# Two transformer blocks on one core: side steps after every three products, and another order of projections

## The chip, the cores and the metric

One core of one Trainium2 chip. The metric is the device time of one execution in microseconds, and lower is better. TensorE multiplies, VectorE and ScalarE work on vectors, SP issues transfers.

## The reference

Two blocks of two layers each, on 256 tokens of width 1024, in float32. Of the first block a layer is a mixer, cross attention with 256 memory rows, and a gated FFN; of the second, an FFN, a mixer with three attentions, and a second FFN. The part that the change is mostly about, cut:

```python
def second_block(x, ...):
    for l in range(DEPTH):
        h = rms_norm_2(x, ffn1_norm[l])
        x = x + 0.5 * swiglu_2(h, ffn1_w_gate[l], ffn1_w_up[l], ffn1_w_down[l])
        h = rms_norm_2(x, mix_norm[l])
        (nq, nkc, nvc, nks, nvs, nkw, nvw, ngate, sq, sk, sv, wq, wk, wv, bgate) = jnp.split(
            h @ w_in[l], SPLIT_POINTS, axis=-1)
        y_nsa = nsa_attention(...)          # sparse: compressed, selected and window branch, 8 heads
        y_sb = stick_breaking_attention(...)  # 4 heads
        y_swa = swa_sink_attention(...)       # sliding window of 128, 4 heads
        g = jax.nn.sigmoid(bgate).reshape(B, S, N_BRANCHES, D_MODEL)
        merged = (g[:, :, 0] * (y_nsa @ w_up_nsa[l]) + g[:, :, 1] * (y_sb @ w_up_sb[l])
                  + g[:, :, 2] * (y_swa @ w_up_swa[l]))
        x = x + merged @ w_out[l]
        h = rms_norm_2(x, ffn2_norm[l])
        x = x + 0.5 * swiglu_2(h, ffn2_w_gate[l], ffn2_w_up[l], ffn2_w_down[l])
    return x
```

In the first block, `parallel_mixer` joins a linear recurrence, a forgetting attention and a retention, all from one projection `h @ w_in`, and `memory_cross_attention` reads keys and values of the memory.

## The kernel before

**Products.** The large matrix products set the pace. Weights are streamed from memory in chunks of up to 1 MB by SP (three raw buffers, `raw`), and each chunk is split into pieces of at most 128x1024: ScalarE rounds a piece to `whi`, VectorE takes the difference `wlo` (six piece buffers). The activations are split alike (`thi`, `tlo`). One product is three matmuls into one PSUM bank, hi·hi, hi·lo and lo·hi, written by `mm3`; in this text a "product" is one such matmul, so `mm3` is three products. A piece in `mm_nat` gives 6 products for each of the two token tiles (two k tiles of 512 columns, or one of 1024), or 12 (four k tiles of 256 columns).

**Side steps.** Everything between the large products, the attentions, the recurrence, the transposes, is written as Python generators. `side(gen)` puts one on a list, and each `yield` ends one step, with the time at which its next one may begin. `pump()` goes through the list and emits the steps that are due, into the same instruction streams, where the program stands. A planner (`Pace`) keeps an estimate of when each engine is done; `pump` takes a step only when its time has come by that estimate (within 0.3 us) and one of two PSUM banks of the pool `aux` is free:

```python
due = [i for i in ready if i[1] <= nc.products + 0.3 and aux_free() <= nc.products + 0.3]
```

Where a product needs what a side step has yet to make, `need` and `finish` call `pump(force=True)`, which emits the next step whether its time has come or not. All engines work through their streams in order, so a side step's instructions stand in TensorE's stream between two products, and its vector work in the streams of VectorE and ScalarE between the splits of weights. The order is settled when the program is built, by the estimate.

**Where `pump()` stands before.** In `nat_blocks`, after every token tile of a piece, so mostly after 6 products; in `stat_block` (weights are the stationary operand there, 128x256 moving) in the middle of each piece and at its end; in `out_rows` after each piece and token tile; in the loop that makes the memory's keys and values (`fill_steps`) in the middle of a piece; in the `up` projections of the second mixer after a piece's second token tile only. The first pass of `nat_blocks` over token tile 0 (`skew`) and the last pieces of `out_rows` (`held`) have none.

**The second mixer.** Its input projection is done in column groups, each a call with a callback, and a callback starts the work on what has come: `nq` (queries of the sparse attention), `sqk` (stick-breaking queries and keys; starts `both`, that is `sb` and then `swa`), `svwq` (stick-breaking values and sliding queries), `nkv` (sparse keys and values for compression and selection; starts `compress_blocks`), `wkv` (sliding keys and values), `nwin` (window keys and values and the gates; starts `nsa`). Then follow the gate projections, between them the compression's matmuls (`compress_mm`, `o<-raw,t`), and three `up` projections. `nsa` has eight units of two heads; `pairs` runs the steps of each unit in turn: scores (`aux<-kT,qT`), softmax rows on VectorE and ScalarE (`rn`), their transposition (`aux<-ident,rn`), the output (`o<-rn,vsw`); after units 4 and 8 the compressed branch's part (`o<-bc,kk`). `swa` has the same steps under the names `wkT,wqT`, `rs`, `wv`. `compress_attention` makes `kc`, `kcb` and that part's probabilities. `ta`, `kk` hold normalised queries and keys on the way to their transposes. The third `up` projection needs the whole output of `nsa` from its third k tile on, the second that of `swa`, the first that of `sb`.

**Cross attention and first mixer** have side steps of their own: `cpr` (probabilities), `o<-cpt,mv` (output), `hk` (strips of the bias table for the second block, read back from memory by a transfer that a side step issues), `rot` (rotated queries), `o<-pt,fv` (forgetting attention).

Of the kernel before, what the change touches and what calls it, by code (L numbers as in the profile page):

```python
# [272 lines left out]
def tile_two_blocks(ctx, tc, I, out):  # L273
# [196 lines left out]
    def mm_nat(dst, T, t, piece, first, last):  # L470

        hi, lo, kts, _ = piece
        b = hi.shape[2]
        for j, kt in enumerate(kts):
            need(T, kt, t)
            xs = slice(t * P, (t + 1) * P)
            for c in range(0, b, 512):
                e = min(c + 512, b)
                mm3(dst(t, c, e), T.hi[:, kt, xs], T.lo[:, kt, xs], hi[:, j, c:e], lo[:, j, c:e],
                    first and j == 0, last and j == len(kts) - 1)  # L480

    def nat_blocks(T, blocks, skew=0, after=None):
# [6 lines left out]
        items = []  # L489
# [5 lines left out]
        def run(item, piece, t):  # L495
            i, n, cb, st = item
            if st["dst"] is None:
                st["dst"] = st["mk"]()
            mm_nat(st["dst"][0], T, t, piece, i == 0, i == n - 1)
            if t == 1 and i == n - 1 and cb:  # L500
                nc.end = nc.products
                cb(st["dst"][1])

        held = []
        for k in range(min(skew, len(items))):
            piece = W.take()
            run(items[k], piece, 0)
            held.append(piece)
            if k in T.late:
                T.late.pop(k)()  # L510
# [19 lines left out]
    def stat_block(T, npieces, ncb, cb, dst=None):  # L530

        a = dst if dst is not None else acc()
        for i in range(npieces):
            piece = W.take()
            hi, lo, kts, idx = piece
            for j, kt in enumerate(kts):
# [10 lines left out]
                if j + 1 == len(kts) // 2:  # L547
                    pump()
# [9 lines left out]
    def out_rows(kt_of, npieces, tail, chain, n_fill=0, both=False, head=0, late=None):  # L558
# [12 lines left out]
        def go(t, T, piece, first, last):  # L571
            mm_nat(dst, T, t, piece, first, last)
            if t == 1:
                W.done(piece[3])

        if head:
            some = [get(i) for i in range(head)]
            for t in (0, 1):
                for k, s in enumerate(some):
                    go(t, *s)  # L580
                    if late and t == 0 and k >= head - 2:
                        next(late)
                    pump()
        for i in range(head, npieces - tail):
            s = get(i)
            for t in (0, 1):
                go(t, *s)
# [603 lines left out]
    def fill_steps(n):  # L1191
# [3 lines left out]
        for l, kind, c in todo:  # L1195
            if kind == "k" or c % 2 == 0:
                a = acc()
            for i in (0, 1):
                hi, lo, kts, idx = W.take()
                for j, kt in enumerate(kts):  # L1200
                    if j == len(kts) // 2:
# [204 lines left out]
    def plan_mixer2(l):  # L1406
# [5 lines left out]
        nat(1304, 512)  # L1412
        nat(1816, 512)
        nat(512, 512)
        nat(2328, 256)
        nat(1024, 280)
# [11 lines left out]
    def mixer2(l, T, next_maker):  # L1428
        with nc.pool(tc, name=nm("mix2"), bufs=2) as mp:
# [426 lines left out]
            nat_blocks(T, [(4, dst_tiles, svwq_done), (4, dst_tiles, nkv_done), (2, dst_tiles, wkv_done), (4, dst_tiles, nwin_done)])  # L1856
# [5 lines left out]
            def up(kt0, n, g0, first):  # L1862
# [3 lines left out]
                for t in (0, 1):  # L1866
                    for i, (hi, lo, kts, idx) in enumerate(held):
                        mm_nat(dst, Y, t, (hi, lo, [kt0 + k for k in kts], idx), i == 0, i == n - 1)
# [201 lines left out]
```

## Time and profile before

| | |
|---|---|
| time, median of 3 runs | 2149.8 us (2143.81 to 2149.81) |
| profiled execution, own time | 2147.57 us |
| its span | 2145.8 us |
| TensorE busy | 2067.2 us (96%) |
| VectorE busy | 1250.7 us (58%) |
| ScalarE busy | 1096.1 us (51%) |
| mean granted clock of TensorE | 0.98 |
| transfers | 380.79 MB, 177 GB/s on the mean |

The own time of the profiled execution is the span of its records and 1.8 us around it. PE is TensorE's matrix multiplication, PEld its weight load, DVE VectorE, ACT ScalarE. [...] A wait is named by what ended it: "aux <- DVE rn" is a matmul into `aux` that waited for VectorE's writing of `rn`. Line L151 is that of the recorder through which the whole program goes; groups are told apart by their tiles.

### The profile page before, as it was taken

To read this page: it belongs to the slowest core of one execution; us is meant where nothing else is said; L and a number is where in the kernel's file an instruction comes from. 1 tells how busy PE (TensorE), PEld (TensorE's weight loads), DVE (VectorE), ACT (ScalarE), POOL (GpSimd) and SP (SyncE) were. 2 spreads that over 40 slices of the span, in tenths; PEclk is the share of its full clock that TensorE was granted. 3 is DMA by queue.
4 is the path that set the end of the run, shared out by engine and by line. 5 is a ranking of instruction groups with operands and counts; after the bars stand their busy time and mean duration, and the time that the engine had idled before them with its cause. 6 is when DMAs were issued, how large, how long until landed. Compare 5 with 4: busy or idle time off the path is not lost.

```text
span 2145.8 us, 27307 instructions
## 1 busy us (share of the span) xinstructions
PE 2067.2 (96%) x10446; PEld 1692.5 (79%) x10446; DVE 1250.7 (58%) x2123; ACT 1096.1 (51%) x1840; POOL 90.2 (4%) x112
## 2 busy tenths in 40 slices
PE   7999999999899999999999999999999998989999
PEld 6878788888787788788887667888888886768887
DVE  6666565556663655565465656664655565647563
ACT  5556465454554654555363545654554454446552
POOL 0210000001100000000000000000000000000000
PEclk9999999999999999999999999999999999989999
DMA  7555565655554555556536543555565547525553
GB/s 241 179 190 179 170 207 177 215 175 164 184 186 149 196 188 195 171 182 204 191 129 197 187 123 138 195 179 195 177 196 189 165 158 225 138 85 194 192 185 109
DMA packets 200610, 380.79 MB, mean 177 GB/s; under 512 B 14288, under 2 KB 70400, under 8 KB 200480
## 3 DMA queue, kind: packets, MB, share of 16 engines
q1 hardware_dynamic: 188960, 366.46, 51.9%
q10 hardware_dynamic: 11520, 12.59, 1.8%
q8 instruction: 82, 1.34, 0.2%
q14 instruction: 48, 0.39, 0.1%
HBM read 372.03 MB, written 6.99 MB: 177 GB/s over the span
## 4 chain that ended last, share of the span: by engine, by line
PE 83%; DVE 6%; ACT 4%; DMA 4%; issue 3%; POOL 1%; SPq 0%; ACTq 0%; DVEq 0%; POOLq 0%
PE acc L151 73%; PE aux L151 7%; DMA raw<-in_w_in_dram 2%; DVE wlo L151 2%; PE o L151 2%; ACT whi L151 1%; ACT rn L151 1%; ACT thi L151 1%; DVE h L151 0%; DMA mem<-in_mem_dram 0%; ACT cpr L151 0%; DMA nb<-cdram 0%; DVE ngm L151 0%; DVE tlo L151 0%; DMA bt<-btiles 0%
## 5 line engine op out<-in xcount | busy, mean ns | idle before, releaser
L151 PE MATMUL acc<-whi,thi 128*128 128x512 f32 (+1 forms) x1760 | 701.5, 399 | 10.8 <-ACT kvout L151 6.5
L151 PE MATMUL acc<-wlo,thi 128*128 128x512 f32 (+1 forms) x1760 | 685.1, 389 | 5.0 <-DVE wlo L151 4.7
L151 PE MATMUL acc<-whi,tlo 128*128 128x512 f32 (+1 forms) x1760 | 685.2, 389 | 2.5 <-DVE tlo L151 2.4
L151 DVE TENSOR_TENSOR wlo<-raw,whi 128x1024 fp32r<-128x1024 f32 (+1 forms) x370 | 442.3, 1208 | 302.1 <-ACT whi L151 300.4
L151 ACT CAST whi<-raw 128x1024 fp32r<-128x1024 f32 (+1 forms) x370 | 378.3, 1036 | 274.1 <-PE acc L151 221.7
L151 DVE SCALAR_TENSOR_TENSOR wlo<-raw,prm,whi 128x512 fp32r<-128x512 f32 (+1 forms) x592 | 392.3, 717 | 178.2 <-ACT whi L151 178.0
L151 ACT ACTIVATE whi<-raw,prm 128x512 fp32r<-128x512 f32 (+1 forms) x592 | 371.6, 694 | 93.3 <-PE acc L151 89.8
L151 PEld LDWEIGHTS acc<-whi,thi 128*128 128x128 f32 x1760 | 333.4, 189 | 88.1 <-issue 11.2
L151 PEld LDWEIGHTS acc<-whi,tlo 128*128 128x128 f32 x1760 | 332.6, 189 | 75.1 <-DVE tlo L151 7.1
L151 PEld LDWEIGHTS acc<-wlo,thi 128*128 128x128 f32 x1760 | 333.5, 189 | 71.4 <-DVE wlo L151 9.1
L151 PE MATMUL acc<-whi,ahi 128*128 128x512 f32 x528 | 206.8, 392 | 0.3
L151 PE MATMUL acc<-whi,alo 128*128 128x512 f32 x528 | 205.6, 389 | 0.0
L151 PE MATMUL acc<-wlo,ahi 128*128 128x512 f32 x528 | 205.5, 389 | 0.0
L151 POOL TENSOR_TENSOR r<-v,mhalf 128x1 f32<-128x1 f32 (+3 forms) x46 | 51.5, 1120 | 1619.5 <-DVE v L151 1619.5
L151 DVE SCALAR_TENSOR_TENSOR silu<-acc,r,silu 128x512 f32<-128x512 f32 (+1 forms) x72 | 47.5, 702 | 118.2 <-PE acc L151 94.2
L151 PEld LDWEIGHTS acc<-whi,ahi 128*128 128x128 f32 x528 | 99.1, 188 | 21.6 <-ACT whi L151 1.5
L151 PEld LDWEIGHTS acc<-whi,alo 128*128 128x128 f32 x528 | 99.1, 188 | 20.6
L151 PEld LDWEIGHTS acc<-wlo,ahi 128*128 128x128 f32 x528 | 99.2, 188 | 20.1
L151 PE MATMUL acc<-thi,whi 128*128 128x256 f32 x384 | 111.7, 291 | 0.0
L151 PE MATMUL acc<-tlo,whi 128*128 128x256 f32 x384 | 108.6, 283 | 0.0
L151 PE MATMUL acc<-thi,wlo 128*128 128x256 f32 x384 | 108.5, 283 | 0.0
L151 ACT ACTIVATE silu<-acc,r 128x512 f32<-128x512 f32 (+1 forms) x72 | 43.1, 650 | 127.7 <-PE acc L151 127.6
(299 smaller groups left out, 1857.1 us busy)
## 6 DMA issues: line engine op xcount, KB each, us to landing
raw<-in_w_in_dram SPq DMA_DIRECT2D x65, 1024.0 KB, 5.0
raw<-in_ffn_w_down_dram SPq DMA_DIRECT2D x44, 1024.0 KB, 4.8
raw<-in_ffn_w_gate_dram SPq DMA_DIRECT2D x40, 1024.0 KB, 5.0
raw<-in_ffn_w_up_dram SPq DMA_DIRECT2D x40, 1024.0 KB, 5.1
raw<-in_w_down_dram SPq DMA_DIRECT2D x22, 1024.0 KB, 4.9
raw<-in_w_gate_dram SPq DMA_DIRECT2D x20, 1024.0 KB, 5.0
raw<-in_w_up_dram SPq DMA_DIRECT2D x20, 1024.0 KB, 5.0
raw<-in_w_out_dram SPq DMA_DIRECT2D x16, 1024.0 KB, 4.9
```

Of the source, the lines that this page charges most:

```text
L151: return f(*args, **kwargs)
```

## The change

Two parts. First, `mm_nat` takes a flag `beside`, with which it calls `pump()` after each three products (not after the last of a piece, which has its own); `nat_blocks` sets it except in its first pass, `out_rows` for all but the held pieces, and `up` throughout. `stat_block` calls `pump()` after each two column blocks, which are six products, and `fill_steps` after each k tile but the last. Second, in the second mixer the projections follow in the order nq, sqk, nkv, nwin, svwq, wkv, instead of nq, sqk, svwq, nkv, wkv, nwin, in the plan of weights and in the calls alike.

```diff
-    def mm_nat(dst, T, t, piece, first, last):
+    def mm_nat(dst, T, t, piece, first, last, beside=False):
...
+        left = len(kts) * (-(-b // 512))
...
+                left -= 1
+                if beside and left:
+                    pump()
...
-        def run(item, piece, t):
+        def run(item, piece, t, beside=True):
...
-            mm_nat(st["dst"][0], T, t, piece, i == 0, i == n - 1)
+            mm_nat(st["dst"][0], T, t, piece, i == 0, i == n - 1, beside)
...
-            run(items[k], piece, 0)
+            run(items[k], piece, 0, False)
...
-                if j + 1 == len(kts) // 2:
-                    pump()
+                    if c % 2 == 1 and (j + 1 < len(kts) or c + 1 < ncb):
+                        pump()
...
-                    go(t, *s)
+                    go(t, *s, beside=True)
...
-                    if j == len(kts) // 2:
+                    if j:
                         pump()
...
+        nat(512, 512)
+        nat(1024, 280)
         nat(1816, 512)
-        nat(512, 512)
         nat(2328, 256)
-        nat(1024, 280)
...
-            nat_blocks(T, [(4, dst_tiles, svwq_done), (4, dst_tiles, nkv_done), (2, dst_tiles, wkv_done), (4, dst_tiles, nwin_done)])
+            nat_blocks(T, [(4, dst_tiles, nkv_done), (4, dst_tiles, nwin_done), (4, dst_tiles, svwq_done), (2, dst_tiles, wkv_done)])
...
-                        mm_nat(dst, Y, t, (hi, lo, [kt0 + k for k in kts], idx), i == 0, i == n - 1)
+                        mm_nat(dst, Y, t, (hi, lo, [kt0 + k for k in kts], idx), i == 0, i == n - 1, True)
```

What this does to the instructions at three places of the second mixer, layer 0. The first is TensorE's stream at the third `up` projection, ahead of its third k tile (`o` is the output of the sparse attention's second half, `acc` the projection). Before:

```order
L151 MATMUL acc_10772<-whi_10652,tlo_9145 128x512
L151 MATMUL aux_10790<-kT_9150,qT_9149 128x128
L151 MATMUL aux_10791<-kT_9150,qT_9149 128x128
L151 MATMUL aux_10790<-kT_9150,qT_9149 128x256
L151 MATMUL aux_10791<-kT_9150,qT_9149 128x256
L151 MATMUL o_10814<-rn_10766,vsw_9148 64x256
L151 MATMUL o_10814<-rn_10768,vsw_9148 64x256
L151 MATMUL o_10814<-rn_10766,vsw_9148 64x128
L151 MATMUL o_10814<-rn_10768,vsw_9148 64x128
L151 MATMUL aux_10819<-ident_90,rn_10798 128x128 x3
L151 MATMUL aux_10820<-ident_90,rn_10803 128x128 x3
```

After the last of these rows two more such units follow, down to the compressed part, before the next product. After the change the same place reads:

```order
L151 MATMUL acc_10889<-whi_10789,thi_9144 128x512
L151 MATMUL acc_10889<-wlo_10790,thi_9144 128x512
L151 MATMUL acc_10889<-whi_10789,tlo_9145 128x512
L151 MATMUL o_10662<-rn_10902,vsw_9148 64x256
L151 MATMUL o_10662<-rn_10904,vsw_9148 64x256
L151 MATMUL o_10662<-rn_10902,vsw_9148 64x128
L151 MATMUL o_10662<-rn_10904,vsw_9148 64x128
L151 MATMUL o_10662<-bc_10569,kk_10425 128x256 x2
L151 MATMUL acc_10889<-whi_10807,thi_9144 128x512
L151 MATMUL acc_10889<-wlo_10808,thi_9144 128x512
```

One output group with the compressed part stands there; the scores, turns and other outputs of these units stand between earlier products.

The second is TensorE's stream at `kc`, `kcb`, the normalised compressed keys, and the sliding attention's `rs`. Before:

```order
L151 MATMUL acc_10331<-whi_10195,thi_9144 128x512
L151 MATMUL acc_10331<-wlo_10196,thi_9144 128x512
L151 MATMUL acc_10331<-whi_10195,tlo_9145 128x512
L151 MATMUL aux_10379<-ident_90,kc_10320 128x30
L151 MATMUL aux_10387<-kcb_10381,qT_9149 128x30 x8
L151 MATMUL aux_10403<-ident_90,rs_10148 128x128 x3
L151 MATMUL aux_10404<-ident_90,rs_10153 128x128 x3
L151 MATMUL o_10250<-rs_10411,wv_9147 64x256
```

Nothing stood between them. After, at `kc` and at `kcb`, which are two pieces of one stream:

```order
L151 MATMUL aux_10456<-ident_90,kc_10428 128x30
L151 MATMUL acc_10322<-whi_10239,thi_8714 128x512
L151 MATMUL acc_10322<-wlo_10240,thi_8714 128x512
L151 MATMUL acc_10322<-whi_10239,tlo_8715 128x512
L151 MATMUL acc_10322<-whi_10239,thi_8714 128x512
L151 MATMUL acc_10322<-wlo_10240,thi_8714 128x512
L151 MATMUL acc_10322<-whi_10239,tlo_8715 128x512
```

```order
L151 MATMUL acc_10322<-whi_10277,thi_8714 128x512
L151 MATMUL acc_10322<-wlo_10278,thi_8714 128x512
L151 MATMUL acc_10322<-whi_10277,tlo_8715 128x512
L151 MATMUL aux_10478<-kcb_10458,qT_9149 128x30 x8
L151 MATMUL acc_10322<-whi_10277,thi_8714 128x512
```

There are 12 products from `kc` to `kcb`, and the groups of `rs` are elsewhere.

The third is VectorE's stream where the sliding attention's queries and keys are normalised (`ta`) ahead of their transposes, with the splits of weights `wlo` for the compress stretch. Before:

```order
L151 TENSOR_REDUCE s_798_9823<-t_795_9799 128x8
L151 TENSOR_SCALAR v_9826<-s_798_9823 128x8
L151 TENSOR_TENSOR wlo_9836<-raw_9797,whi_9835 128x1024
L151 TENSOR_TENSOR wlo_9852<-raw_9797,whi_9851 128x1024
L151 TENSOR_TENSOR ta_9776<-wqk_9491,r_793_9779 128x768
L151 TENSOR_TENSOR kk_9610<-kk_9610,r_799_9824 128x512
L151 TENSOR_SCALAR wqT_9151<-aux_9877,prm 128x2x128
L151 TENSOR_SCALAR wkT_9152<-aux_9877,prm 128x128
```

After:

```order
L151 TENSOR_SCALAR rn_9871<-rn_9871,nsum_9864 128x128
L151 TENSOR_SCALAR rn_9871<-rn_9871,nsum_9864 128x256
L151 TENSOR_TENSOR ta_9824<-wqk_9701,r_808_9827 128x768
L151 TENSOR_TENSOR wlo_9921<-raw_9883,whi_9920 128x1024
L151 TENSOR_SCALAR wqT_9151<-aux_9942,prm 128x2x128
L151 TENSOR_SCALAR wkT_9152<-aux_9942,prm 128x128
L151 TENSOR_TENSOR wlo_9955<-raw_9883,whi_9954 128x1024
```

The multiplication into `ta` stood behind two splits of one chunk and stands ahead of them now.

Counted over the whole program, places with side steps on TensorE's stream go from 239 to 276; in a second mixer, from 38 to 52 in each layer. Places where only three products separate two groups of side steps were none and are 11 in each second mixer, 3 and 5 in the first mixers. In an FFN one place moves by three products.

## Rows read from the trace of the kernel before

**Rows 1.** The page: the span, and busy time of each engine.

```profile
span 2145.8 us, 27307 instructions
...
PE 2067.2 (96%) x10446; PEld 1692.5 (79%) x10446; DVE 1250.7 (58%) x2123; ACT 1096.1 (51%) x1840; POOL 90.2 (4%) x112
```

**Rows 2.** Windows of eight stretches: busy time of each engine, granted clock, DMA.

```profile
696.00:885.80 189.80, 188.04 (x852) 154.01 (x851) 109.18 (x151) 100.90 (x155) 2.69 (x4) 1.00 0.56 186
1075.90:1325.60 249.70, 233.77 (x1258) 181.65 (x1258) 150.24 (x318) 121.04 (x232) 9.57 (x9) 0.95 0.49 156
1272.90:1294.90 22.00, 16.55 (x80) 9.75 (x78) 7.84 (x44) 9.10 (x32) 0.00 (x0) 0.69 0.05 16
1220.60:1232.40 11.80, 8.10 (x40) 6.49 (x38) 8.09 (x23) 2.14 (x5) 0.00 (x0) 0.67 0.29 91
1158.90:1166.30 7.40, 4.41 (x29) 1.90 (x27) 6.04 (x9) 2.50 (x3) 0.00 (x0) 0.78 0.67 223
1898.10:1921.40 23.30, 17.88 (x81) 10.54 (x79) 7.84 (x44) 9.15 (x32) 0.00 (x0) 0.63 0.05 14
582.50:592.50 10.00, 6.02 (x29) 3.60 (x27) 4.50 (x11) 3.71 (x9) 0.00 (x0) 0.69 0.32 122
659.70:672.10 12.40, 8.69 (x26) 5.70 (x24) 2.24 (x3) 2.72 (x5) 0.00 (x0) 0.72 0.70 233
```

**Rows 3.** Waits of TensorE by what ended them: us in total, times, longest.

```profile
PE aux L151 <- DVE rn L151: 9.3, 6, 2.3
...
PE aux L151 <- DVE ta L151: 6.0, 2, 3.0
PE aux L151 <- DVE kcb L151: 5.8, 2, 2.9
PE acc L151 <- DVE wlo L151: 4.7, 8, 0.8
PE aux L151 <- DVE cpr L151: 3.8, 2, 3.0
PE aux L151 <- DMA hk<-ud: 3.7, 1, 3.7
...
PE aux L151 <- ACT rs L151: 1.8, 2, 0.9
```

**Rows 4.** TensorE's timeline, end of the second mixer, layer 0: start, us, instruction.

```profile
1273.18 0.93 PE L151 MATMUL aux<-kT,qT 64*128 64x128 f32 x8
...
1277.18 1.16 PE L151 MATMUL aux<-ident,rn 128*128 128x128 f32 x6 [2.27 <-DVE rn L151]
...
1294.90 0.50 PE L151 MATMUL acc<-whi,thi 128*128 128x512 f32 x1 [0.68 <-ACT thi L151]
```

**Rows 5.** TensorE's timeline, second mixer, layer 0: three side groups between products.

```profile
1201.21 0.39 PE L151 MATMUL acc<-whi,tlo 128*128 128x512 f32 x1
1201.44 0.82 PE L151 MATMUL aux<-ident,rn 128*128 128x128 f32 x6
...
1202.33 0.39 PE L151 MATMUL acc<-wlo,thi 128*128 128x512 f32 x1
...
1209.18 0.39 PE L151 MATMUL acc<-whi,tlo 128*128 128x512 f32 x1
1209.50 0.93 PE L151 MATMUL aux<-kT,qT 64*128 64x128 f32 x8
...
1210.69 0.39 PE L151 MATMUL acc<-wlo,thi 128*128 128x512 f32 x1
...
1266.18 0.39 PE L151 MATMUL acc<-whi,tlo 128*128 128x512 f32 x1
1266.50 0.87 PE L151 MATMUL o<-rn,vsw 128*64 128x256 f32 x8
1267.30 1.13 PE L151 MATMUL o<-bc,kk 128*128 128x256 f32 x4
...
1268.50 0.40 PE L151 MATMUL acc<-wlo,thi 128*128 128x512 f32 x1
```

More of the change, by code (lines that the diff above doesn't have):

```diff
@@ L569, in get, with go @@
             return T, (hi, lo, [k - base for k in kts], idx), i == 0, i == npieces - 1
-        def go(t, T, piece, first, last):
-            mm_nat(dst, T, t, piece, first, last)
+        def go(t, T, piece, first, last, beside=False):
+            mm_nat(dst, T, t, piece, first, last, beside)
             if t == 1:
@@ L586, in out_rows @@
             for t in (0, 1):
-                go(t, *s)
+                go(t, *s, beside=True)
                 pump()
```

## The prediction

> **What bounds the kernel now.** Read the page first [rows 1]: TensorE is busy 2067.2 of 2145.8 us, so 78.6 us of the span are waits, and the rest can only shrink where TensorE ran at its lower clock. The question is then where these two lie. The windows [rows 2] answer it. In an FFN stretch (the first row) TensorE is busy 188.04 of 189.80 us at a granted clock of 1.00: nothing to win. In the second mixer of block two (second row) it is busy 233.77 of 249.70 at 0.95, and the rows of short stretches below it say which parts lower that mean: 22.0 us at 0.69, 11.8 at 0.67, 7.4 at 0.78 and, in layer 1, 23.3 at 0.63. In each of these stretches no product runs: several side steps stand one behind the other, and TensorE waits between them for the step before. [...] The list of TensorE's waits [rows 3] names the same places: 9.3 us for `rn` (rows of scores after the softmax, on VectorE), 6.0 for `ta`, 5.8 for `kcb`, 3.8 for `cpr`, 3.7 for a transfer of `hk`. The timeline of the 22 us stretch [rows 4] shows one such wait: the scores start at 1273.18, their transpose can only start at 1277.18 after 2.27 us idle, and the first product comes back at 1294.90.
>
> So the bound is TensorE, and what can be won is waiting for chains VectorE–ScalarE–TensorE that have no products to cover them.
>
> **The change, part by part.** No matmul is removed. It makes more places where side steps may stand, and it brings the sparse attention's inputs forward by one or two projections (sqk, then nkv and nwin before svwq and wkv). The order of the instructions says what becomes of the stretches.
>
> *End of the second mixer.* Before, the last `up` projection, at its third k tile, needs what four units of the sparse attention have still to give, and ten groups are forced there in a row; after, only the last output group stands there (the rows are in the part on the change). At full clock, what stays of the stretch is its matmuls. Their price is read where such groups stand between products at full clock [rows 5]: time from the last product before to the second product behind, less two pitches of a product (1201.44 less 1201.21, 0.23). Scores: 1210.69 − 1209.18 − 0.46 = 1.05. Turns: 1202.33 − 1201.21 − 0.46 = 0.66. Output with the compressed part: 1268.50 − 1266.18 − 0.46 = 1.86. For an output group alone I take the price of the scores, which have as many matmuls: 1.05. The stretch has 3 scores, 3 turns, 4 outputs, one of them with the compressed part: 3 × 1.05 + 3 × 0.66 + 3 × 1.05 + 1.86 = 10.1 us. These stay, elsewhere. So does the wait of 0.68 for `thi` at its end [rows 4]. Gain: 22.0 − 10.1 − 0.7 = 11.2 in layer 0 and 23.3 − 10.1 − 0.7 = 12.5 in layer 1: **23.7**.
>
> *Compressed attention* (one place before, with `kc`, `kcb`, two groups of the sliding attention's `rs` and one of `rn`; `kc` and `kcb` stand apart after). For this and the next stretches I take busy time times granted clock as the work that stays [rows 2]; on the stretch above that gives 16.55 × 0.69 = 11.4 where the prices gave 10.1, so it errs toward too small a gain. 11.8 − 8.10 × 0.67 = 6.4, twice (two layers): **12.8**. The wait for `kcb`, 2.9 each, is in it; 12 products (2.7 us) stand between `kc` and `kcb` after, so about nothing of that wait is left.
>
> *The compress stretch with* `ta`. 7.4 − 4.41 × 0.78 = 4.0, twice: **8.0**. In VectorE's order `ta`'s multiplication stood behind two splits `wlo` before and stands ahead of them after, which takes the wait of 3.0 away.
>
> *A smaller wait* of the sliding scores for a bank that ScalarE reads (`rs`, 0.9 in each layer) lies where the order now has other products ahead: **1.8**.
>
> *Block one.* First mixer, layer 1: 10.0 − 6.02 × 0.69 = **5.8**. Cross attention, layer 1: 12.4 − 8.69 × 0.72 = 6.1; its wait of 3.7 is for a transfer, which is issued by a side step too and may only move, so I take **5**. Layer 0: of the two waits for `cpr`, 3.8, the large one, **3.0**, since by the order 12 products now stand between that step and the scores ahead of it.
>
> *What is late next.* The sliding attention's inputs now come last. By the order its output group stands 60 products (13.6 us) ahead of the `up` projection that needs it, so nothing is charged. The moved steps issue transfers too: the bias tiles on ScalarE's queue, one unit (some 8 us in the stretch above) ahead of their use, and three small ones on SP's queue between weights that lead by several pieces: nothing either.
>
> FFN stages: one side position per layer moves by three products; **0**, covered by products at clock 1.00 on both sides.
>
> Sum of gains: 23.7 + 12.8 + 8.0 + 1.8 + 5.8 + 5 + 3 = 60.1 us.
>
> **What it adds.** Positions with side steps go from 239 to 276, and in 30 places only three products (0.68 us) are left between two groups of one chain: turn, copy by ScalarE, output. None such existed before, so the trace has no price. Below: nothing, if the copy is done within the three products. Above: the longest wait for such a copy, 0.9 (rs, [rows 3]), thus 0 to 27 us. I take 0.3 each, nearer to the lower end, because the products in between are cover that the stretches of before did not have: 9. The 37 new positions have edges of their own; the scores' 1.05 against their 0.93 of busy time gives some 0.1 more: 0 to 8, taken as 3, since a good part stood alone already. Weight halves late: eight waits for `wlo` now, 0.8 the longest [rows 3]; side steps move ahead of splits in VectorE's queue, so I count two more a layer in the second mixer at 0.8: 3. `kc` stands three products behind its inputs' step: 1 a layer, 2 (0 to 5). Added: 17.
>
> Net 60.1 − 17 = 43; the busy-times-clock terms count too much work by about a tenth (1.3 of 11.4 in the one stretch with both), which is 3 us of the 28 so counted, and makes 46. 2147.6 (the profiled execution's own time) − 46 = **2101**. The median of the runs, 2149.8, is 0.1% above that execution.
>
> **Rivals.**
>
> *A grid with less slack* (14%). Before, a side step that became ready between two positions waited for the next, mostly 6 products on; that delay was also slack for its data. After, it is taken at once when the planner thinks its input done (to within 0.3 us). Some 144 groups move (40 a layer in the second mixers, 24 and 19 in the first, 9 and 12 in cross). If the planner is 0.2 us too early on each, 29 us come back: 2130. For it: TensorE waited six times for `rn`, 9.3 us [rows 3], so steps do come ahead of VectorE's work. Against: those in the stretch of rows 4 were forced steps, and the three groups which the planner placed freely in rows 5 waited for nothing.
>
> *The clock does not come back* (8%). Of the gain, busy × (1 − clock) is clock: 5.1 and 6.6 at the mixer's end, 2 × 2.7, 2 × 1.0, 1.9 and 2.4, together 23. If the small matmuls lower the clock also between products, that stays lost: 2124. Against it: the product behind the six turns at 1201.44 has the duration of the one before them, 0.39, the full clock's. [...]
>
> *No new waits at all* (10%): 2147.6 − 60.1 − 3 = 2084.
>
> *The weights' transfers bound it* (4%). The compress stretch has a DMA share of 0.67 where its stage has 0.49 [rows 2], so weights may be what comes last there; if the 8.0 are only turned into a wait for them, 2109, inside the likeliest range.
>
> *Slower* (4%). Splits of weights stand in the same queues of VectorE and ScalarE as the side steps; the more of those are put between products, the later a split comes. By the order, 29 pieces a layer are split between the compress stretch and the mixer's end, 58 in all. At 0.8 us a piece (the longest `wlo` wait so far) the 46 are given back; at 1.0, 2101 + 58 = 2159. Against: eight such waits in the whole trace, 4.7 us together. [...]
>
> *The change does not do what it says*: excluded for the mixers by the order of instructions, true for the FFNs alone, where nothing is counted.
>
> **The numbers.** Likeliest, 60%: 2085 to 2116, at 2101. A range of 2078 to 2128 leaves out the slower case, the outer part of the grid's rival and half of the tail below. Faster by over 0.3% (which is about what a measurement of this kernel can tell from no change, 6 us): all but the slower rival and a few per cent near nothing: 0.93; same 0.03; slower 0.04.
>
> **What would show it.** Right: the four stretches at the lower clock in the second mixers gone, their windows at 0.98 or more, waits for `rn`, `ta`, `kcb` together under 5 us instead of 21.1; the second mixers about 18 us shorter each, block one 10 us; the FFN windows unchanged. Wrong by the grid: many waits of 0.2 to 0.8 on ScalarE's `rn`/`rs` copies and VectorE's softmax rows. Wrong by the clock: waits gone but windows still below 0.9. Wrong by the weights: waits for `wlo` and `whi` of over 10 us in all. If the mixer's end still shows more than one unit behind the last product, the planner's due times, not the positions, were what held the steps.

## The result and the profile after

The changed kernel takes 2095.6 us (median of four runs, 2092.55 to 2099.48) against 2149.81 before (four runs): a ratio of 0.9753, with a 95% interval of 0.9727 to 0.9779. It is faster by 2.5%, 54 us, and lies 5 us below the predicted 2101. The profiled execution took 2099.48 us, the slowest of the four, 48.1 us less than the one of before, where the prediction, which reckoned from that one, had 46.

The page of the changed kernel, to be read beside [rows 1]:

```profile
span 2097.7 us, 27293 instructions
...
PE 2040.0 (97%) x10446; PEld 1673.8 (80%) x10446; DVE 1251.1 (60%) x2123; ACT 1096.9 (52%) x1842; POOL 92.7 (4%) x112
```

TensorE's busy time fell by 27.2 us, although it has the same 10446 matmuls: this is read as what came back from the lower clock, whose mean over the span went from 0.98 to 0.996. The span fell by 48.1, so that 20.9 us are waits that went (78.6 before, 57.7 after). The granted clock is given as a share of full speed. In the kernel before, at the last `up` projection of layer 0, it reads 1.00 ahead of the stretch and 0.50 inside it (columns of [rows 2]):

```profile
1263.00:1272.90 9.90, 9.90 (x56) 7.54 (x52) 5.33 (x17) 6.12 (x14) 0.00 (x0) 1.00 0.64 225
1283.00:1290.00 7.00, 5.71 (x24) 3.59 (x25) 3.03 (x18) 2.82 (x10) 0.00 (x0) 0.50 0.00 0
```

Windows of the changed kernel, in the columns of [rows 2]: an FFN, the second mixer of layer 0 and of layer 1, the stretch at the last `up` projection (22.0 us in [rows 2]), and a stretch with a new wait:

```profile
678.90:869.00 190.10, 188.34 (x853) 154.35 (x852) 109.30 (x151) 100.90 (x155) 2.66 (x4) 1.00 0.56 186
1059.30:1294.30 235.00, 224.46 (x1259) 175.54 (x1259) 149.48 (x317) 121.21 (x233) 10.48 (x9) 0.99 0.53 166
1668.80:1904.40 235.60, 222.87 (x1258) 174.41 (x1258) 149.29 (x317) 120.93 (x233) 10.49 (x9) 0.99 0.52 166
1260.20:1263.10 2.90, 2.23 (x14) 1.16 (x12) 0.20 (x2) 0.63 (x2) 0.00 (x0) 1.00 0.14 58
1144.20:1148.20 4.00, 0.97 (x5) 0.55 (x4) 0.94 (x1) 2.02 (x4) 0.00 (x0) 0.92 1.05 371
```

The FFN is as it was. In the second mixers the granted clock is 0.99, where it was 0.95 in layer 0, and the stretch at the end holds 2.9 us at full clock. TensorE's timeline of that place, to be held against [rows 4]:

```profile
1260.17 0.40 PE L151 MATMUL acc<-whi,tlo 128*128 128x512 f32 x1
1260.50 0.87 PE L151 MATMUL o<-rn,vsw 128*64 128x256 f32 x8
1261.30 1.13 PE L151 MATMUL o<-bc,kk 128*128 128x256 f32 x4
1263.11 0.50 PE L151 MATMUL acc<-whi,thi 128*128 128x512 f32 x1 [0.68 <-ACT thi L151]
```

One output group with the compressed part, then the product, and the wait of 0.68 for `thi` that was left in the sum. What TensorE waits for now (us in total, times, longest), in the lines that the next parts speak of:

```profile
PE aux L151 <- ACT rn L151: 7.6, 2, 4.5
PE aux L151 <- DVE rs L151: 4.5, 2, 2.6
PE aux L151 <- DMA hk<-ud: 3.8, 2, 2.6
PE acc L151 <- ACT kvout L151: 2.7, 2, 1.8
...
PE acc L151 <- DVE wlo L151: 2.6, 5, 0.8
...
PE aux L151 <- DVE cpr L151: 0.3, 2, 0.2
```

VectorE's `rn`, `ta` and `kcb` of [rows 3] are gone from it as things waited for, `cpr` is down from 3.8 to 0.3. In their place stand 7.6 us for ScalarE's copies of `rn` and 4.5 for VectorE's `rs`; the strips `hk` are waited for as before.

Where the time came from is best read by stage: the time from the first transposition of one stage's input on TensorE to that of the next stage's, in the profiled execution of each run (the first stage from the start of the span, the last to its end). The first row is in us, the others are differences to it; the six FFNs stand together.

| run | mixer 1, l. 0 | cross, l. 0 | mixer 1, l. 1 | cross, l. 1 | mixer 2, l. 0 | mixer 2, l. 1 | FFNs |
|---|---|---|---|---|---|---|---|
| before | 182.1 | 81.0 | 157.5 | 82.4 | 249.6 | 251.9 | 1141.2 |
| changed | −7.4 | −1.1 | −9.0 | +0.3 | −14.6 | −16.3 | 0.0 |
| changed, again | −7.7 | −1.1 | −10.4 | −0.2 | −16.0 | −15.8 | +0.2 |
| e1: places, old order | −7.2 | −1.1 | −11.3 | −1.9 | −10.5 | −12.3 | +0.1 |
| e2: order, old places | −1.9 | +1.6 | 0.0 | −0.2 | −14.3 | −17.4 | +0.1 |
| e6: order, new places in block one alone | −8.1 | −1.1 | −9.0 | −0.1 | −15.4 | −15.7 | 0.0 |
| e8: without the places in stationary blocks | −1.4 | +1.4 | +1.2 | −0.9 | −15.9 | −16.2 | +0.1 |
| e3: places after each product | −2.3 | −1.1 | −9.7 | −0.2 | −14.4 | −16.3 | +1.1 |
| e4: compression weights spread | −6.0 | −1.1 | −10.9 | −1.3 | −13.5 | −15.5 | +0.2 |
| e5: half of the compression weights | −8.6 | −1.1 | −9.0 | −0.4 | −16.3 | −17.7 | 0.0 |
| e7: strips two steps ahead | −7.5 | −1.1 | −11.3 | −5.1 | −16.3 | −18.1 | +0.2 |
| e9: four raw buffers, five pieces | −3.5 | −1.0 | +2.3 | −1.1 | −18.4 | −18.4 | +2.9 |
| e10: e7 with old places in half of mixer 2 | −7.4 | −1.1 | −11.1 | −5.1 | −16.1 | −18.6 | 0.0 |
| e11: extra transposes in the last FFN | −7.4 | −1.0 | −10.9 | −1.4 | −16.0 | −18.3 | +43.1 |

The two profiles of the changed kernel differ by up to 1.4 us in a stage, and the first mixer of layer 1, whose instructions are the same in the changed kernel, e1 and e7, ranges over 2.3 us: a difference between stages of one profile below some 2 us is not read as an effect.

### The profile page after: what moved, and what is told of

Its sections match the earlier page's. It is cut to its first block, busy times and chain, and to the rows that moved or that the text cites. A ratio compares the mean times of both kernels' runs of the same rounds, so it can differ in the third digit from the quotient of the medians.

```text
span 2097.7 us, 27293 instructions
## 1 busy us (share of the span) xinstructions
PE 2040.0 (97%) x10446; PEld 1673.8 (80%) x10446; DVE 1251.1 (60%) x2123; ACT 1096.9 (52%) x1842; POOL 92.7 (4%) x112
## 4 chain that ended last, share of the span: by engine, by line
PE 82%; DVE 7%; ACT 4%; DMA 4%; issue 2%; POOL 1%; SPq 0%; ACTq 0%; DVEq 0%; POOLq 0%
PE acc L151 74%; PE aux L151 7%; DVE wlo L151 3%; DMA raw<-in_w_in_dram 2%; PE o L151 2%; ACT whi L151 2%; DMA hk<-ud 1%; ACT thi L151 1%; DVE h L151 0%; ACT cpr L151 0%; DVE rs L151 0%; DVE t L151 0%; DMA mem<-in_mem_dram 0%; DVE ngm L151 0%; DMA nb<-cdram 0%
## 5 line engine op out<-in xcount | busy, mean ns | idle before, releaser
L151 ACT ACTIVATE silu<-acc,r 128x512 f32<-128x512 f32 (+1 forms) x72 | 43.1, 650 | 127.7 <-PE acc L151 127.6
```

Of the source, the lines that this page charges most:

```text
L151: return f(*args, **kwargs)
```

## The experiments

**Which part does what (e1, e2, e6).** In e1 the four lines of the plan and the list of blocks are put back:

```diff
-        nat(512, 512)
-        nat(1024, 280)
         nat(1816, 512)
+        nat(512, 512)
         nat(2328, 256)
+        nat(1024, 280)
...
-            nat_blocks(T, [(4, dst_tiles, nkv_done), (4, dst_tiles, nwin_done), (4, dst_tiles, svwq_done), (2, dst_tiles, wkv_done)])
+            nat_blocks(T, [(4, dst_tiles, svwq_done), (4, dst_tiles, nkv_done), (2, dst_tiles, wkv_done), (4, dst_tiles, nwin_done)])
```

> The changed kernel with the old order of projections; the new places for side steps stay. Theory (the places do most of it, the order only moves the last units of the sparse attention out of the stretch at the last up projection): by the order of instructions that stretch holds five groups instead of ten before and two in the changed kernel, so some 9 us of its 22 are kept in each layer; block one is as in the changed kernel, 17 us shorter than before. About 2110 us, ratio to before 0.981. Rival (the order of projections carries the second mixers, the places only block one): 2150 - 17 - 4 = 2129 us.

Measured: 2104.2 us against 2145.8, ratio 0.9806 (0.9791 to 0.9820). That is nearer to the theory's 2110 than to its rival's 2129; whether the places do most of it in the second mixers is for the next run. The end of the second mixer and the whole mixer of layer 0, as windows:

```profile
1253.00:1263.00 10.00, 7.00 (x37) 4.00 (x35) 2.82 (x16) 3.52 (x12) 0.00 (x0) 0.83 0.03 11
1052.00:1292.00 240.00, 227.68 (x1262) 178.08 (x1261) 149.30 (x318) 120.96 (x233) 10.11 (x10) 0.96 0.51 163
```

Ten us at clock 0.83 are left of the 22.0 at 0.69: forced steps of one unit still stand there. In the second mixers the places alone win 22.8 us.

In e2 the kernel before has the new order and nothing else (the same lines, the other way round).

> The kernel before with the new order of projections only; side steps stand where they stood. Theory: block one and the FFNs unchanged; in the second mixers the stretch at the last up projection keeps seven of its ten groups, and the one at kc, kcb, rs is as it was, so some 6 us a layer are won, with the wait for ta gone but a wait for weights in its place: about 2137 us, ratio 0.994. Rival (the order is what matters in the second mixers): 2150 - 31 = 2119 us. Rival (the order by itself gives nothing): 2150 us.

Measured: 2117.8 us against 2145.8, ratio 0.9867 (0.9852 to 0.9882). The rival is right: the order wins 31.7 us in the second mixers, all that the whole change wins there (30.9), and block one is as it was. The theory's reason, that the places do most of it, fails with that: it counted the groups that are left at the end, and missed what they cost. TensorE's timeline of that place in e2:

```profile
1267.12 0.39 PE L151 MATMUL acc<-whi,tlo 128*128 128x512 f32 x1
...
1268.71 1.16 PE L151 MATMUL aux<-ident,rn 128*128 128x128 f32 x6 [0.40 <-DVE rn L151]
...
1274.28 1.16 PE L151 MATMUL aux<-ident,rn 128*128 128x128 f32 x6 [2.07 <-DVE rn L151]
...
1277.43 2.08 PE L151 MATMUL o<-bc,kk 128*128 128x256 f32 x4
1280.19 0.50 PE L151 MATMUL acc<-whi,thi 128*128 128x512 f32 x1 [0.67 <-ACT thi L151]
```

Seven groups are still forced (with the compressed part as one; so counted they were eleven before), in 13.1 us instead of 22.0, with two waits for `rn`, 0.40 and 2.07, instead of the 2.27 of [rows 4] and two more. The stretch at `kcb` shrank as well, from 11.8 to 6.6 us, without any new place for it.

In e6 block one and the FFNs have the new places, the second mixers' projections the old ones, and the order is the new one:

```diff
-    def nat_blocks(T, blocks, skew=0, after=None):
+    def nat_blocks(T, blocks, skew=0, after=None, fine=True):
...
-        def run(item, piece, t, beside=True):
+        def run(item, piece, t, beside=fine):
...
-            nat_blocks(T, [(4, dst_tiles, nq_done)], skew=4)
-            stat_block(T, 4, 4, sqk_done)
+            nat_blocks(T, [(4, dst_tiles, nq_done)], skew=4, fine=False)
+            stat_block(T, 4, 4, sqk_done, fine=False)
```

and so on for the mixer's other calls, `up` included.

> The changed kernel with the old places for side steps in the second mixers' projections, and the new order of projections; block one keeps the new places. By the order of instructions its second mixers read as in the run with the new order only, its block one as in the changed kernel. Theory (in the second mixers the new order is enough and the new places add nothing): second mixers 235 and 235 us, block one 17 us shorter than before, ratio 0.975 to 0.977, the same as the changed kernel. Rival (the new places are worth something there beside the order): 2100 us or more, ratio 0.979 and above.

Measured: 2097.9 us against 2147.8, ratio 0.9768 (0.9750 to 0.9787); the changed kernel beside it gave 0.9757 (0.9737 to 0.9777). The second mixers win 31.0 us without the new places in their projections, and TensorE's order in them is that of e2. So in them the two parts are two ways to the same gain, and the order is the better one.

**Which places count in block one (e8).** The places after each three products stay, those in `stat_block` and in the loop for the memory's keys and values are put back to the middle of a piece:

```diff
-                    if c % 2 == 1 and (j + 1 < len(kts) or c + 1 < ncb):
-                        pump()
+                if j + 1 == len(kts) // 2:
+                    pump()
...
-                    if j:
+                    if j == len(kts) // 2:
                         pump()
```

> The changed kernel with the old places in the blocks whose weights stand in TensorE and in the memory's keys and values (one in the middle of a piece); the places after each three products and the new order stay. Theory (in the first mixers both kinds of place count: by the order of instructions the last block there keeps two of its three or four groups behind the last product): some 5 us of the first mixers' 17 are lost in each layer where that block stands, second mixers as in the changed kernel: about 2101 us, ratio 0.979. Rival (only the places after each three products count): no change, 0.976.

Measured: 2114.1 us against 2145.9, ratio 0.9850 (0.9836 to 0.9865). More is lost than either said: of block one's 17.2 us nothing is left (the four stages are 0.3 us longer than before, together), and the second mixers keep theirs. TensorE's waits in e8:

```profile
PE acc L151 <- ACT kvout L151: 3.9, 2, 2.9
PE aux L151 <- DVE cpr L151: 3.8, 2, 3.0
PE aux L151 <- DMA hk<-ud: 3.5, 1, 3.5
...
PE o L151 <- DVE rvg L151: 3.1, 1, 3.1
...
PE aux L151 <- DVE rot L151: 2.6, 3, 1.3
```

The waits for `cpr` and `rot` are back at about their sizes before (3.8 and 2.8), with part of that for `kvout`; that for `hk` had never gone, and one for `rvg` is new. In layer 1 it isn't the stretch of 10.0 us of [rows 2] that came back: another, of 8.1 us without products, stands earlier in the stage, with the wait for `rvg`. So the places after each three products win nothing in block one by themselves. Which of the two kinds that e8 puts back, in `stat_block` or in `fill_steps`, wins the 17, and whether they win it alone, was not tried.

**A finer grid still (e3).** A place after each single product, in the same calls:

```diff
         mm(ps, xhi, whi, start=start, stop=False)
+        if beside:
+            pump()
         mm(ps, xhi, wlo, start=False, stop=False)
+        if beside:
+            pump()
```

> The changed kernel with a place for side steps after each single product instead of each three, in the same calls. Theory (a finer grid costs no slack; what waits are left come from weights and from chains): by the order of instructions no group is left at the last up projection, worth 1 to 2 us a layer, and waits move little: 2088 to 2098 us. Rival (a finer grid takes slack away, each moved group waits some 0.2 us more): over 100 groups move again, 20 us: 2115 us.

Measured: 2104.6 us against 2145.8, ratio 0.9804 (0.9788 to 0.9820): between the two, 9 us slower than the changed kernel by the medians. The second mixers don't move, so no slack is lost there, and no gain is left either. The loss is in the first mixer of layer 0 (5 us; one stretch of 8 us with `rvg`, `rot` and `rqkT` stands there without products) and 0.2 us in each FFN. Neither theory had that.

**The waits for ScalarE's `rn` in the compress stretch (e4, e5, e9).** The trace of the changed kernel shows how they come about; all engines, layer 1, start and duration:

```profile
1748.32 1.03 ACT L151 CAST whi<-raw 128x1024 fp32r<-128x1024 f32 x1
...
1749.38 1.23 DVE L151 TENSOR_TENSOR wlo<-raw,whi 128x1024 fp32r<-128x1024 f32 x1 [1.97 <-ACT whi L151]
...
1750.63 0.37 SPq L151 DMA_DIRECT2D raw<-in_w_in_dram  x1
...
1752.58 0.82 PE L151 MATMUL aux<-ident,rn 128*128 128x128 f32 x6
...
1753.72 0.40 PE L151 MATMUL acc<-whi,tlo 128*128 128x512 f32 x1
1757.17 1.04 ACT L151 CAST whi<-raw 128x1024 fp32r<-128x1024 f32 x1 [7.82 <-DMA raw<-in_w_in_dram]
1758.12 0.85 ACT L151 COPY rn<-aux 128x384 f32<-128x384 f32 x2
...
1758.64 0.90 PE L151 MATMUL aux<-ident,ta 128*128 128x128 f32 x3 [4.53 <-ACT rn L151]
```

`ta` (TensorE, 1758.64) waits for a bank of `aux`, which ScalarE has yet to empty by its copies of `rn`. These are queued behind a cast of weights, `whi`, which waits 7.82 us for its chunk. The chunk was only issued at 1750.63, when VectorE's split at 1749.38 was done with its predecessor, and took 6.5 us to land. The copies' input was ready at about 1753.4 (the transposes of 1752.58 and their 0.82), while ScalarE stood idle in those 7.82 us; they ran right behind the cast, at 1758.12, 4.7 us later.

e4 spreads the four chunks of compression weights over four gate projections:

```diff
-        for c, kv in ((0, "k"), (512, "v")):
-            for k in (0, 1):
-                W.plan(w, 2584 + D + c, 2584 + D + c + 512, 4 * k, 4 * k + 4, 4, 2)
-                W.plan(I[f"nsa_cmp_{kv}_w1_2"][l], 0, 256, 8 * k, 8 * k + 8, 8, 4, split=False)
-        gates(2)
+        for i in range(8):
+            c0 = 2584 + (1 + i // 4) * D + 512 * (i // 2 % 2)
+            W.plan(w, c0, c0 + 512, 4 * (i % 2), 4 * (i % 2) + 4, 4, 2)
+            if i % 2:
+                kv, k = "kkvv"[i // 2], i // 2 % 2
+                W.plan(I[f"nsa_cmp_{kv}_w1_2"][l], 0, 256, 8 * k, 8 * k + 8, 8, 4, split=False)
```

> The changed kernel with the four chunks of compression weights spread over four gate projections instead of two: one after each two chunks of gate weights instead of one after each. Theory (the waits for rn, 3.0 and 4.5 us, and for rs, 1.9 and 2.6 us, in the compress stretch of the changed kernel are late transfers of weights, handed on through ScalarE's queue): these 12 us go; by the order of instructions five groups instead of two are left at the last up projection, since the compressed branch is later, which costs some 5 us a layer: 2093 us, and the windows of the compress stretch without those waits. Rival (the waits are the side steps' own, whatever the weights do): the waits stay, 2105 us.

Measured: 2097.2 us against 2145.8, ratio 0.9770 (0.9755 to 0.9785). Its waits of these kinds:

```profile
PE o L151 <- ACT t L151: 5.8, 2, 2.9
PE aux L151 <- DVE rn L151: 4.5, 2, 2.3
...
PE aux L151 <- ACT rn L151: 0.6, 2, 0.3
```

The 12 us for ScalarE's `rn` and VectorE's `rs` shrank to 0.6, as the theory has it, but 5.8 for `t` (the bank of the compression's matmuls, which ScalarE copies into `t`) and 4.5 for `rn` at the last `up` projection came instead: the place changed, the time didn't.

e5 halves what is loaded, with every instruction where it was:

```diff
-                W.plan(I[f"nsa_cmp_{kv}_w1_2"][l], 0, 256, 8 * k, 8 * k + 8, 8, 4, split=False)
+                W.plan(I[f"nsa_cmp_{kv}_w1_2"][l], 0, 128, 8 * k, 8 * k + 8, 8, 4, split=False)
...
-                            mm(a[32 * j : 32 * j + 32, k * S : k * S + S], blocks[:, k, kt, :], w[:, j, :], i == 0, i == 3, beside=j > 0)
+                            mm(a[32 * j : 32 * j + 32, k * S : k * S + S], blocks[:, k, kt, :], w[:, j, :].unsqueeze(1).to_broadcast([P, 2, P]), i == 0, i == 3, beside=j > 0)
```

> The changed kernel with half of each of the four chunks of compression weights left unloaded (the other half's columns are used twice, so that part of the computation is not the reference's); every engine's instructions stand in the same order as in the changed kernel. Theory (late transfers of weights cause the waits of ta for ScalarE's copies of rn, 3.0 and 4.5 us, and of the turns of rs for VectorE, 1.9 and 2.6 us): these 12 us become less than 4. Rival (the waits are due to the place of the side steps): they stay at 10 us or more.

Measured (one execution): 2094.5 us; the waits:

```profile
PE aux L151 <- ACT rn L151: 6.2, 2, 3.1
PE aux L151 <- DVE rs L151: 4.5, 2, 2.6
```

10.7 us are left of 12.1, and e7 below, with the same order of instructions and all of the weights, has 10.3. So the amount of compression weights is not what makes the chunk late. What is left is that it is issued late: of the three raw buffers two then hold compression weights, which are used where they are and come free only after their matmuls (SP's next issue, of another such chunk, stands at 1751.91, behind the matmuls that read the first, 1750.78 and their 1.07). e9 has four raw buffers, and five piece buffers to make room:

```diff
-NPIECE = 6
-NRAW = 3
+NPIECE = 5
+NRAW = 4
```

> The changed kernel with four buffers for raw weights instead of three, and five for split pieces instead of six (there is no room for both). Theory (in the compress stretch two of three raw buffers hold compression weights, so that the next chunk of gate weights is issued only when the last one is split, and ScalarE's queue stands until it lands): the waits for ScalarE's copies of rn and for VectorE's rs, 12 us in both layers of the changed kernel, fall below 4, and ScalarE's longest wait for a raw chunk there falls from 7.8 to under 3. What five pieces cost elsewhere is open, so the total is 2085 to 2105 us. Rival (the transfer itself is too slow): the waits stay at 10 us or more.

Measured: 2106.8 us against 2145.9, ratio 0.9804 (0.9785 to 0.9824). ScalarE's waits for a chunk of the projections' weights, first in the changed kernel, then in e9:

```profile
ACT whi L151 <- DMA raw<-in_w_in_dram: 32.5, 12, 7.8
```

```profile
ACT whi L151 <- DMA raw<-in_w_in_dram: 4.2, 3, 3.4
```

TensorE's list in e9 names neither ScalarE's `rn` nor VectorE's `rs` any more; behind the wait for `h` at the start it begins with

```profile
PE acc L151 <- DVE wlo L151: 9.9, 12, 1.6
...
PE acc L151 <- ACT whi L151: 6.1, 6, 2.4
```

The second mixers are 2 to 4 us shorter than in the changed kernel. More is lost elsewhere: waits of products for `wlo` and `whi` are 16.0 us in all (3.0 in the changed kernel), and the first mixers are 4 and 11 us longer than there, the FFNs 2.9. The fourth buffer brings the chunks in time, and the remedy is too dear. It does not show that the buffers alone make the wait: the planner moved side steps as well in e9, and e6 and e10, with three buffers and the old places in the compress stretch, have no wait for ScalarE's `rn` either (4.1 and 4.0 us for `wkT` instead), and ScalarE waits 4.2 and 4.5 us at the longest for a chunk. It takes both, a chunk that is issued late and side steps that stand behind its cast.

The chunk was late before the change too. ScalarE and VectorE in the kernel before, layer 0, at the wait for `ta`:

```profile
1158.49 1.99 ACT L151 CAST whi<-raw 128x1024 fp32r<-128x1024 f32 x2 [5.85 <-DMA raw<-in_w_in_dram]
...
1159.57 2.36 DVE L151 TENSOR_TENSOR wlo<-raw,whi 128x1024 fp32r<-128x1024 f32 x2 [4.25 <-ACT whi L151]
1161.84 0.95 DVE L151 TENSOR_TENSOR ta<-wqk,r 128x768 f32<-128x768 f32 x1
```

The splits ahead of `ta` waited for casts, and these 5.85 us for their chunk: TensorE's 3.0 us for `ta` were a transfer's under another name, as the 7.6 for `rn` are.

**The strips `hk` (e7).** Loaded two steps ahead instead of one:

```diff
-            hk = bp.tile([P, 2, S], F32, tag="hk", name=nm("hk"))
+            hk = bp.tile([P, 2, S], F32, tag="hk", name=nm("hk"), bufs=3)
...
         load(0)
+        load(2)
         for h in range(0, 12, 2):
-            if h + 2 < 12:
-                load(h + 2)
+            if h + 4 < 12:
+                load(h + 4)
```

> The changed kernel with the strips hk loaded two steps ahead instead of one (three buffers instead of two); TensorE's instructions stand in the same order. Theory (the cross attention of layer 1 gained nothing because a strip's transfer takes 5 us and the steps follow at 2.5 us or less): the two waits of 3.8 us in all go, with some 2 us of lower clock behind them: that stage 5 us shorter, the total 2091 us. Rival (the transfers wait in the queue behind weights, whenever they are issued): the waits stay within 1 us and so does the time.

Measured: 2090.3 us against 2147.8, ratio 0.9745 (0.9720 to 0.9770). The list of TensorE's waits no longer names `hk`, and the cross attention of layer 1 is 5.1 us shorter than before, where the changed kernel gained nothing. As expected; of the time as a whole the intervals of e7 and of the changed kernel overlap, so the gain is read from this stage, which lies between +0.3 and −1.9 in the other runs, which load one strip in advance, e10 aside.

**The changed kernel once more**, beside e5, e6 and e7:

> The changed kernel once more, beside the others of this call: 2092 to 2099 us as measured before, and the same waits for ta, rs and hk as in its first profile; how far its stages differ from the first profile tells how well a stage of one profile can be read.

Measured: 2094.8 us, ratio 0.9757 (0.9737 to 0.9777); the waits for `rn` 7.8, for `rs` 4.4, for `hk` 3.5.

**Both, and the places only where they might help (e10).** e7, and in the second mixers the old places up to the compress stretch, the new ones from the third gate projection on (as in e6, with `fine=False` on the first four calls alone).

> The changed kernel with the strips hk two steps ahead, and in the second mixers the old places up to and with the compress stretch, the new places from the third gate projection on. Theory (early places there put steps ahead of late weights; late places clear the last up projection): the waits for ta go, the stretch at kc, kcb is spread, three groups are left at the end: second mixers 2 us shorter each than in the changed kernel, and with 5 us from the strips 2086 us, ratio 0.972. Rival (what the one half of the mixer wins the other loses): 2091 us, 0.974, as with the strips alone.

Measured: 2086.7 us against 2145.9, ratio 0.9719 (0.9705 to 0.9734), the fastest of the kernels here. The time is the theory's; the stages speak for the rival: the second mixers are as in e7 (−16.1 and −18.6 against −16.3 and −18.1), so that what is clear of the noise in its gain over the changed kernel is that of the strips. The intervals of e10 and e7 overlap, and the runs don't settle more. The waits for ScalarE's `rn` are gone, others of their size (4.0 for `wkT`, 3.4 for `bc`, 2.8 for VectorE's `rn`) have come.

**Transposes and the clock (e11).** In the last FFN, behind each place for side steps, three transposes that nobody reads (`turns` counts the FFNs):

```diff
                 if beside and left:
                     pump()
+                    if turns[0] == 6:
+                        ps = aux()
+                        for i in range(3):
+                            turn(ps[:, i * P : (i + 1) * P], ident, ident)
```

> The changed kernel with 120 extra groups of three transposes (128x128, of a constant, read by nobody) between products of the last FFN, one behind each place for side steps there. Theory (the lower clock comes from stretches without products, not from transposes between them): the granted clock of that stage stays at 1.00, each group costs 0.3 to 0.4 us, the stage is 36 to 48 us longer than its 193 us. [...]

Measured (one execution): 2135.6 us. The window of that FFN:

```profile
1904.00:2133.80 229.80, 225.36 (x1185) 184.06 (x1183) 99.67 (x131) 87.87 (x126) 0.00 (x0) 1.00 0.42 137
```

The clock is 1.00 over this window, the stage 43.1 us longer, 0.36 us for each of the 120 groups. The transposes between products did not lower the clock here. That the stretches of [rows 2] had the lower clock for want of products fits this; no run parts the want of products from the waits that stand in the same stretches.

## Why the prediction was right, and where its steps were not

The mechanism was right: the stretches without products went, and with them waits and the lower clock. The total was 5 us off, its parts further, and that they cancelled was luck: about 36 us were forecast for the second mixers and 10 for block one, 30.9 and 17.2 were measured in the first profile.

- **End of the second mixer (23.7).** Right: the stretch went from 22.0 to 2.9 us and from 23.3 to 2.9 in layer 1 (the 1870.33 to 1873.27 of its timeline); less the work that moved, 10.1 − 1.9 = 8.2 each, that is 10.9 and 12.2, together 23.1. The 8.2 are the prediction's own prices, which no run measured by themselves.
- **`kc`, `kcb` (12.8).** Right in place: no wait for `kcb` is left, and products stand between `kc` and `kcb`. What it gave was not measured by itself; in e2 the order alone took the stretch from 11.8 to 6.6 us.
- **The compress stretch (8.0).** This step failed: "which takes the wait of 3.0 away" is true of VectorE's multiplication, but TensorE then waited 3.0 and 4.5 us in the same place for ScalarE, and 1.9 and 2.6 a little later for `rs`: 12.1 us instead of 6.0. The step took the two splits ahead of `ta` for the cause, where the splits themselves waited for a late chunk. The rival "the weights' transfers bound it" had the place and about the price, with too small a chance (4%); e5, e6, e9 and e10 show what it takes, a chunk issued late and side steps behind its cast.
- **The smaller wait (1.8).** That of the scores for ScalarE's `rs` is gone from TensorE's list.
- **Cross attention, layer 1 (5).** Failed, in the way that its own sentence named: the wait only moved, 3.7 before and 3.8 after, and the stage gained nothing. e7 shows what was missing: one strip more in advance.
- **Cross attention, layer 0 (3).** Too large: the wait for `cpr` went from 3.0 to 0.2, but the stage gained 1.1. TensorE's busy time in it rose by 1.1 us.
- **First mixers (5.8 in layer 1, nothing in layer 0).** Too small: 9.0 and 7.4. That layer 0 was put at nothing had no reason. TensorE's list of before has one more large wait, which [rows 3] does not show:

```profile
PE acc L151 <- ACT kvout L151: 6.5, 2, 4.2
```

The 4.2 for `kvout` lie in layer 0, where 1.0 is left of them; in all this wait fell from 6.5 to 2.7. By e8 the gain hangs on the places in `stat_block` and `fill_steps`.
- **What it adds (17).** No run measures the sum; two of its terms can be checked. The 30 gaps of three products cost nothing that the list of waits shows (9 were counted; no wait of an output group for a copy is in it). Late weights cost 12 instead of 3 (of which the 6.0 for `ta` had been theirs before), and by ScalarE's and VectorE's queues rather than at the products: TensorE's own waits for `wlo` fell from 4.7 to 2.6.
- **The second mixers' sum.** About 18 us each were forecast, 14.6 and 16.3 measured (16.0 and 15.8 in the second profile). Against the 8.0 that the compress stretch was to give stand the 12.1 us of new waits there.
- **Rivals.** "The clock does not come back" is excluded: 27.2 us of TensorE's busy time went, and e11 has 120 groups of transposes between products at clock 1.00. "A grid with less slack" did not happen at three products: e6, without them in the second mixers, is no faster. At one product (e3) 9 us were lost, but not there. "Slower" by late splits did not happen: what waited was the other way round, side steps behind a late cast, 12 us.

What the prediction did not do is to part the two edits. The runs do: in the second mixers the order alone gives everything, and the places after each three products, the largest part of the diff, show no gain of their own in any run with the new order; block one's gain needs those in `stat_block` and `fill_steps`, of one kind or both.

## What to carry to other kernels

Where an engine stands in forced steps, first ask whether their inputs can be made earlier: in the second mixers the order alone gave 31.7 us, the finer grid alone 22.8, both together 30.9. Before a wait is priced, follow its chain past the engine that it is named by: here `ta`, then splits, then casts, then a late chunk of weights; and a strip's transfer of 5.2 us (the median of six in the changed kernel) for steps that may follow after 2.5. Read the whole list of waits, too: `kvout`, the third largest, was in no term. And price a change of several edits edit by edit, even when the diff has one purpose.

## What the runs showed of the hardware that was not expected

Against the prediction's rival on the clock, 120 groups of three 128x128 transposes between the products of one FFN left the granted clock at 1.00, at 0.36 us each (e11, which expected so). And a wait for a transfer stood in the profile under the name of a ScalarE copy into which it was handed on: of the 7.6 us "ACT rn" the larger wait, 4.5, was a chunk of weights issued 6.5 us before it landed. Halving the compression weights took no more from the 12.1 us (10.7 left) than one execution of the same order differs from another (e7, 10.3).
